# A decoder step on one core: the head that builds the modulated input is rebuilt, and index queries are projected only from token 256 on

## The chip, the core and the metric

The kernel runs on one core of a Trainium2 chip. Its time is the device time of one execution in microseconds (us). Before the change three runs gave a median of 1173.57 us, from 1172.87 to 1173.94. The engines are called PE (TensorE, matrix products), DVE (VectorE), ACT (ScalarE), POOL (GpSimd) and SP (SyncE, which issues nearly all DMAs). PSUM holds what PE writes, SBUF everything else. A line number such as L209 is a line of the kernel before; lines of the kernel after are always called so.

## The reference, cut to what matters

The step takes 1024 new prompt tokens and 8 sequences of 4 sample tokens, 1056 in all, each a row of 1024 values.

```
mod = silu(c) @ w_ada + b_ada                     # c: 9 conditioning rows
shift, scale, gate = split(mod, 3)
r = rsqrt(mean(x*x) + 1e-6)                       # one norm factor per token
h = (x * r) * g_norm * (1 + scale) + shift
qa, ka, va, za, qi, ki, wi, qr, kr, vr, zr, ga, gr = split(h @ w_in)
# index scores: sum over 4 heads of relu(qi . ki) * wi; 256 best keys per query, causal
# attention of qa over the chosen ka, va; times silu(za)
# retention (qr, kr with rotary, vr, decay per head, chunks of 128), group norm, times silu(zr)
merged = sigmoid(ga) * (y_a @ w_pa) + sigmoid(gr) * (y_r @ w_pr)
y = rms_norm(x + gate * (merged @ w_out), g_final)
```

A query at position below 256 has at most 256 admissible keys, so for it all of them are chosen and its index scores decide nothing. Sample tokens also take part, with 1024 cached keys and their own.

## The kernel before, in words

All of h is held transposed, channels on partitions, tokens along the row: 8 tiles of 128 channels (index k) by 1056 tokens. Each fp32 value is split into a high and a low part (`HH[k]`, `HL[k]`), and so is each weight (`wh`, `wl`). A projection of 128 output columns is, for each of 3 chunks of 352 tokens and each k, three products: wh·HH, wh·HL, wl·HH (`terms`, L206 to L211), 72 in all.

The stages are these. **The head** (L232 to L340) loads the constants `C` (128x792), the rows of x (one sample block, 8 prompt blocks) and the weights `wa` of the modulation, two 512 KB loads for each k. Each block of x is squared on ACT with a sum per row (L285); after three blocks a reciprocal root is taken on DVE, the block is scaled by it on DVE or POOL (L292), transposed on PE (L295) and copied from PSUM on ACT and DVE (L297). For each k `h_tile` multiplies the conditioning by `wa` (PE, L203), copies (ACT, L305), sums by another product (L308), forms scale AA and shift BB on DVE (L309, L310), applies them to the 1024 prompt columns in one instruction (L312) and to the 32 sample columns in two (L315), casts HH on ACT (L316) and subtracts for HL on DVE or POOL (L317). `start_two` runs inside that: two projections at once (index keys KI with the head weights, and the first 128 index query columns QI), 18 products for each k in six PSUM banks, with their weights split on POOL (L222, L223).

**The index stage** then copies these results out, transposes the keys (L627), projects the other 128 query columns (`project(O_QI + 128, ...)`), and scores queries from token 256 on against keys (L645, L646; combined on DVE, L652), then the sample tokens against the cache. ACT's copy L712 of the sample scores is the last input of the **selection**.

**The selection** (`pick_all`) searches a threshold bit by bit: 31 rounds in which DVE counts five blocks (L728) and ACT two (L735), with a few tiny DVE instructions per round (L742, L804, L806), followed by exact tie handling and a mask for each block (L780 to L784). It shares DVE with the gates' projections and with **retention**, four pairs of heads one after the other; each pair has a recurrence of seven DVE steps over S (L489), read by PE in L508. Attention for samples, attention for prompt tokens and the output follow.

The order on each engine is not written out: a scheduler simulates a timeline while the program is built and places instructions by it; pools with few buffers and `tc.issue_after` edges (an order on one engine, not a wait of its own) restrict it. At run time each engine works its list in that order.

Of the kernel before, what the change touches and what calls it, by code (L numbers as in the profile page):

```python
# [30 lines left out]
SQD = ()  # L31
SEQ = (8, 0, 1, 2, 3, 4, 5, 6, 7)
GRP = (0, 3, 6, 9)
CP = 0
PH = (2, 4, 6)
# [84 lines left out]
def _hybrid_step(ctx, tc, A, outs, dbg):  # L120
# [26 lines left out]
    nc.sync.dma_start(C, A["cst"])  # L147
# [34 lines left out]
    gT = cst.tile([128, 4], F32, name="gT")  # L182
    
# [15 lines left out]
    def ada_rows(x, w):  # L199

        for k in range(KT):
            q = k % 4
            nc.tensor.matmul(x[32 * q:32 * q + 32], scT[:, k], w[:, k], start=(k < 4), stop=(k >= 4))  # L203
# [11 lines left out]
    def start_two(pool, f0, f1):  # L215

        banks = [pj()[:, :CH] for _ in (0, 1)] + [x[:, o:o + CH] for x in (pl(), pl()) for o in (0, 512)]
        W = []
        for f in (f0, f1):
            ws = wload(wp, w_in, f, 128)  # L220
            wh, wl = [pool.tile([128, KT, 128], F32R, name="x", bufs=9) for _ in "hl"]
            nc.gpsimd.tensor_scalar(wh, ws, 1.0, 1.0, op0=OP.mult, op1=OP.mult)  # L222
            nc.gpsimd.tensor_sub(wl, ws, f32(wh))  # L223
            W.append((wh, wl))
        for k in range(KT):
            for i, p in enumerate(banks):
                terms(p, W[i // 3], k, chunks[i % 3])
        return banks
# [3 lines left out]
    with ExitStack() as s0:  # L232
        sp = s0.enter_context(tc.tile_pool(name="sp", bufs=1, reuse_waits="tile"))
        NWA = 5
        warm = sp.tile([1, 1], F32, name="warm")
        nc.vector.memset(warm, 0.0)
        nc.scalar.activation(warm, warm, AF.Tanh)
        craw, th = [sp.tile([128, D], F32, name="wa", bufs=NWA)[:9] for _ in (0, 1)]
        nc.scalar.dma_start(craw[0:1], A["c_prompt"])
        nc.scalar.dma_start(craw[1:9], A["c_sample"])  # L240
        rows = sp.tile([48, 128], F32, name="rows")
# [5 lines left out]
        ssq = sp.tile([128, 9], F32, name="ssq")  # L247
        nc.vector.memset(ssq, 1.0)
        XR = sp.tile([128, KT, TT], F32, name="xr")
        AA = sp.tile([128, KT, 9], F32, name="AA")  # L250
        BB = sp.tile([128, KT, 9], F32, name="BB")
        X = {}

        def x_load(t):
            n = 128 if t < 8 else NS
            X[t] = sp.tile([128, D], F32, name="x", bufs=9)
            nc.sync.dma_start(X[t][:n], xp[t * 128:t * 128 + 128] if t < 8 else xs)

        def cond():
# [11 lines left out]
            nc.vector.tensor_scalar(cols[:, 8:16], cols[:, 8:16], 1.0, None, op0=OP.add)  # L271
            nc.vector.tensor_copy(gT, cols[:, 32:36])

        def x_blocks(i0, i1):

            size = lambda t: 128 if t < 8 else NS
            for i in range(i0, i1):
                t = SEQ[i]
                n, x = size(t), X[t]
                sq = sp.tile([128, D], BF, name="sq", bufs=2)  # L280
                if t in SQD:
                    nc.vector.tensor_tensor_reduce(out=sq[:n], in0=x[:n], in1=x[:n], scale=1.0, scalar=0.0,
                                                   op0=OP.mult, op1=OP.add, accum_out=ssq[:n, i:i + 1])
                else:
                    nc.scalar.activation(sq[:n], x[:n], AF.Square, accum_out=ssq[:n, i:i + 1])  # L285
# [3 lines left out]
            for i in range(i0, i1):  # L289
                t = SEQ[i]  # L290
                n, x = size(t), X[t]
                (nc.vector if t % 2 else nc.gpsimd).tensor_scalar(x[:n], x[:n], r[:n, i - i0:i - i0 + 1], 1.0, op0=OP.mult, op1=OP.mult)  # L292
                p = pl().rearrange("p (k t) -> p k t", k=KT)
                for k in range(KT):
                    nc.tensor.transpose(p[:, k, :n], x[:n, 128 * k:128 * k + 128], ident[:n, :n])  # L295
                for g, copy in ((slice(0, 4), nc.scalar.copy), (slice(4, 8), nc.vector.tensor_copy)):
                    copy(XR[:, g, t * 128:t * 128 + n], p[:, g, :n])  # L297

        def h_tile(k, w2):

            pm = pt()
            for o, w in enumerate(w2):
                ada_rows(pm[:, 128 * o:128 * o + 128], w)
# [5 lines left out]
            nc.vector.tensor_scalar(AA[:, k], pm[:, 16:25], cols[:, 8 + k:9 + k], cols[:, 24 + k:25 + k], op0=OP.add, op1=OP.mult)  # L309
            nc.vector.tensor_scalar(BB[:, k], pm[:, 0:9], cols[:, k:k + 1], None, op0=OP.add)  # L310
            h = XR[:, k, :T]
            nc.vector.tensor_scalar(h, h, AA[:, k, 0:1], BB[:, k, 0:1], op0=OP.mult, op1=OP.add)  # L312
            hs = XR[:, k, T:].rearrange("p (b i) -> p b i", b=NB)
            for op, ab in ((OP.mult, AA), (OP.add, BB)):
                nc.vector.tensor_tensor(hs, hs, ab[:, k, 1:9].unsqueeze(2).to_broadcast([128, NB, NI]), op=op)  # L315
# [3 lines left out]
        wa = {}  # L319

# [983 lines left out]
```

## Time and profile before

| what | value |
|---|---|
| median of 3 runs | 1173.57 us |
| profiled execution, its own time | 1169.95 us |
| span of its trace | 1168.1 us |
| mean granted clock of TensorE | 0.98 |
| PE busy | 1104.2 us (95%) |
| DVE busy | 669.1 us (57%) |
| ACT busy | 452.8 us (39%) |
| POOL busy | 329.6 us (28%) |

The busy times are sums over a span of stages with different limits, and matmul records overlap, so PE's 95% says only that it is rarely without work. The profile's row of 40 slices shows for PE a 4 in the first slice and nines nearly everywhere else; DVE has nines and eights from the sixth slice to the fifteenth, and is far lower behind. The profiled execution is 3.6 us shorter than the median of the runs.

### The profile page before, as it was taken

To read this page: it belongs to the slowest core of one execution; us is meant where nothing else is said; L and a number is where in the kernel's file an instruction comes from. 1 tells how busy PE (TensorE), PEld (TensorE's weight loads), DVE (VectorE), ACT (ScalarE), POOL (GpSimd) and SP (SyncE) were. 2 spreads that over 40 slices of the span, in tenths; PEclk is the share of its full clock that TensorE was granted. 3 is DMA by queue.
4 is the path that set the end of the run, shared out by engine and by line. 5 is a ranking of instruction groups with operands and counts; after the bars stand their busy time and mean duration, and the time that the engine had idled before them with its cause. 6 is when DMAs were issued, how large, how long until landed. Compare 5 with 4: busy or idle time off the path is not lost. (4 is left out here: it accounts for less than half of the span.)

```text
span 1168.1 us, 20306 instructions
## 1 busy us (share of the span) xinstructions
PE 1104.2 (95%) x8040; PEld 1008.5 (86%) x8040; DVE 669.1 (57%) x1599; ACT 452.8 (39%) x874; POOL 329.6 (28%) x258
## 2 busy tenths in 40 slices
PE   4999999999989959999998999999999999989997
PEld 3899989999879959999998999877888888888786
DVE  6865349999999998113332222211237767477755
ACT  5465445555555311222243333212326666343211
POOL 2413006023311700160332222053114433376000
PEclk9999999999999987999999999999999999999999
DMA  9913234145222422341687567589889841395221
GB/s 306 255 33 109 74 105 139 38 126 140 84 79 93 148 58 80 101 120 29 220 269 237 178 205 213 154 294 305 266 245 237 233 135 55 123 299 176 106 97 54
DMA packets 157892, 181.51 MB, mean 155 GB/s; under 512 B 18837, under 2 KB 129501, under 8 KB 156710
## 3 DMA queue, kind: packets, MB, share of 16 engines
q1 hardware_dynamic: 147864, 144.51, 41.7%
q0 software_dynamic: 9856, 35.66, 9.2%
q8 instruction: 63, 1.03, 0.4%
q14 instruction: 31, 0.25, 0.1%
q10 hardware_dynamic: 78, 0.06, 0.0%
HBM read 137.81 MB, written 38.60 MB: 151 GB/s over the span
## 5 line engine op out<-in xcount | busy, mean ns | idle before, releaser
L209 PE MATMUL pj<-hh,wh 128*128 128x352 f32 x1176 | 387.7, 330 | 7.6 <-ACT kx L395 3.0
L211 PE MATMUL pj<-hh,wl 128*128 128x352 f32 x1176 | 383.1, 326 | 0.0
L210 PE MATMUL pj<-hl,wh 128*128 128x352 f32 x1176 | 382.6, 325 | 0.0
L209 PEld LDWEIGHTS pj<-hh,wh 128*128 128x128 f32 x1176 | 223.0, 190 | 17.1 <-issue 6.0
L210 PEld LDWEIGHTS pj<-hl,wh 128*128 128x128 f32 x1176 | 223.7, 190 | 3.3 <-issue 2.5
L211 PEld LDWEIGHTS pj<-hh,wl 128*128 128x128 f32 x1176 | 223.0, 190 | 3.9 <-issue 3.4
L728 DVE TENSOR_SCALAR_CACHE_REDUCE eq<-sc,cand 128x896 bf16<-128x896 f32 (+4 forms) x155 | 135.7, 875 | 2.3
L196 POOL TENSOR_TENSOR wl<-ws,wh 128x1024 fp32r<-128x1024 f32 (+1 forms) x33 | 63.6, 1930 | 190.9 <-ACT wh L195 172.6
L195 ACT CAST wh<-ws 128x1024 fp32r<-128x1024 f32 (+1 forms) x65 | 61.1, 940 | 108.4 <-PE pj L210 66.9
L196 DVE TENSOR_TENSOR wl<-ws,wh 128x1024 fp32r<-128x1024 f32 x32 | 39.9, 1247 | 86.8 <-ACT wh L195 86.8
L1065 POOL TENSOR_SCALAR lg<-lg,st 128x1024 f32<-128x1024 f32 (+7 forms) x64 | 47.5, 749 | 75.3 <-DVE st L1064 69.6
L735 ACT ACTIVATE ra<-sc,cand 128x1024 bf16<-128x1024 f32 x31 | 35.6, 1149 | 64.9 <-DVE cand L806 64.9
L911 POOL DMA_INDIRECT kv<-in_cache_k,idx x32 | 30.9, 966 | 102.0 <-PE str L941 84.0
L1063 ACT ACTIVATE lg<-lg,st 128x1024 f32<-128x1024 f32 (+7 forms) x64 | 49.5, 775 | 21.4 <-DVE st L1062 21.2
L943 DVE COPY kt<-str 128x512 f32<-128x512 f32 x32 | 22.1, 689 | 61.3 <-PE str L941 57.6
L911 POOL DMA_INDIRECT kv<-in_cache_v,idx x32 | 31.4, 981 | 71.0 <-PE sx L969 41.8
L1241 PE MATMUL pj<-wol,MH 128*128 128x512 f32 (+1 forms) x136 | 51.2, 377 | 0.0
L1240 PE MATMUL pj<-woh,MH 128*128 128x512 f32 (+1 forms) x136 | 51.2, 377 | 0.0
L1242 PE MATMUL pj<-woh,ML 128*128 128x512 f32 (+1 forms) x136 | 51.2, 377 | 0.0
L574 ACT ACTIVATE raw<-pj 128x352 f32<-128x352 f32 x48 | 22.1, 460 | 71.9 <-PE pj L211 68.7
L1078 PE MATMUL tr<-C,lg 128*128 128x128 f32 x288 | 43.8, 276 | 1.3 <-ACT pT L1080 0.5
L1078 PEld LDWEIGHTS tr<-C,lg 128*128 128x128 f32 x288 | 33.7, 140 | 8.7 <-ACT pT L1080 1.9
(337 smaller groups left out, 2055.6 us busy)
## 6 DMA issues: line engine op xcount, KB each, us to landing
ws<-in_w_in SPq DMA_DIRECT2D x51, 512.0 KB
TG<-raw SPq DMA_DIRECT2D x16, 528.0 KB
rot<-in_rot SPq DMA_DIRECT2D x8, 1056.0 KB
wa<-in_w_ada SPq DMA_DIRECT2D x16, 512.0 KB
u<-TG SPq DMA_DIRECT2D x8, 528.0 KB
RT<-u SPq DMA_DIRECT2D x8, 528.0 KB
t<-TG SPq DMA_DIRECT2D x8, 528.0 KB
u<-RT SPq DMA_DIRECT2D x8, 528.0 KB
```

Source lines behind the costliest of these rows:

```text
L195: nc.scalar.copy(wh[:, :, :n], ws[:, :, :n])
L196: (nc.vector if len(order) % 3 else nc.gpsimd).tensor_sub(wl[:, :, :n], ws[:, :, :n], f32(wh[:, :, :n]))
L209: nc.tensor.matmul(p, wh[:, k], HH[k][:, sl], start=(k == 0), stop=False)
L210: nc.tensor.matmul(p, wh[:, k], HL[k][:, sl], start=False, stop=False)
L211: nc.tensor.matmul(p, wl[:, k], HH[k][:, sl], start=False, stop=(k == KT - 1))
L728: nc.vector.tensor_scalar(junk[:n, :W], sc, thr[:n, j:j + 1], 0.0, op0=op, op1=OP.add, accum_out=cnt[:n, j:j + 1])
L911: nc.gpsimd.indirect_dma_start(out=t.rearrange("p s c -> p (s c)"), out_offset=None, in_=cache.rearrange("g (r s) h d -> (g r) (s h d)", s ...
L1063: nc.scalar.activation(l, l, AF.Exp, bias=st[:, 2:3], scale=0.125, accum_out=st[:, 3:4])
L1078: nc.tensor.transpose(x[:, 128 * (j - j0):128 * (j - j0) + 128], lg[:, j % 2, 128 * (j // 2):128 * (j // 2) + 128], ident)
L1240: nc.tensor.matmul(x, MH[:, k, tk], wh[:, k], start=(k == 0), stop=False)
L1241: nc.tensor.matmul(x, MH[:, k, tk], wl[:, k], start=False, stop=False)
L1242: nc.tensor.matmul(x, ML[:, k, tk], wh[:, k], start=False, stop=(k == KT - 1))
```

## The change

In the head, raw rows of x are transposed as they land and copied out unscaled. The squares are taken on ACT, except blocks 1 and 4, which DVE takes. The norm factors come in two groups (five blocks, then four); each is put on the diagonal of a 128x128 tile, and a product of a matrix of ones with that tile spreads it over all partitions into `RB`, so that norm and scale are applied to the transposed tile in one DVE instruction. The shift is added where HH is cast (ACT) and HL formed (DVE), each in two halves of 528 columns. AA and BB move to ACT. Nothing in the head runs on POOL. Of the constants only the identity is loaded ahead of x, the other 664 columns behind it. The weights of the two first projections are loaded behind the first pair of `wa` and split on ACT and DVE; later weights are ordered behind the last `wa` load and the last HH and HL. The six products of a term become five: three of 352 columns for KI, two of 400 for the queries (tokens 256 to 655, 656 to 1055), and a term runs over all five before the next. The second block of query columns uses the same two pieces.

```diff
-GRP = (0, 3, 6, 9)
-PH = (2, 4, 6)
+SQD = (1, 4)
-    nc.sync.dma_start(C, A["cst"])
+    nc.sync.dma_start(C[:, :C_CAUS], A["cst"][:, :C_CAUS])
+    late = [slice(256, 656), slice(656, TT)]
+    def start_two(W):
+        x, y = pl(), pl()
+        parts_ = [(p[:, :sl.stop - sl.start], sl, i) for p, sl, i in
+                  zip((pj(), pj(), x[:, :512], x[:, 512:], y[:, :512]), chunks + late, (0, 0, 0, 1, 1))]
         for k in range(KT):
-            for i, p in enumerate(banks):
-                terms(p, W[i // 3], k, chunks[i % 3])
+            for term in range(3):
+                for p, sl, i in parts_:
+                    nc.tensor.matmul(p, W[i][term == 2][:, k], (HL if term == 1 else HH)[k][:, sl], ...)
+        part = lambda: sp.tile([128, D], F32, name="x", bufs=11)
+        def x_block(i):
+            for k in range(KT):
+                nc.tensor.transpose(p[:, k, :n], x[:n, 128 * k:128 * k + 128], ident[:n, :n])
+            if t in SQD: nc.vector.tensor_tensor_reduce(out=sq[:n], in0=x[:n], in1=x[:n], ...)
+            else: nc.scalar.activation(sq[:n], x[:n], AF.Square, accum_out=ssq[:n, i:i + 1])
+            for g, copy in ((slice(0, 4), nc.scalar.copy), (slice(4, 8), nc.vector.tensor_copy)):
+                copy(XT[:, g, t * 128:t * 128 + n], p[:, g, :n])
+        def norms(i0, i1):
+            r = rsqrt(sp, v, i1 - i0)
+            for i in range(i1 - 4, i1):
+                nc.vector.tensor_scalar(dg, ident, r[:, i - i0:i - i0 + 1], None, op0=OP.mult)
+                nc.tensor.matmul(p[:, o:o + 128], one, dg, start=True, stop=True)
+            nc.scalar.copy(RB[:, c0:c0 + 512], p)
+            ...
-            h = XR[:, k, :T]
-            nc.vector.tensor_scalar(h, h, AA[:, k, 0:1], BB[:, k, 0:1], op0=OP.mult, op1=OP.add)
-            nc.scalar.copy(HH[k], XR[:, k])
-            (nc.gpsimd if k in PH else nc.vector).tensor_tensor(HL[k], XR[:, k], f32(HH[k]), op=OP.subtract)
+            nc.scalar.activation(AA[:, k], pm[:, 16:25], AF.Identity, bias=cg[:, k:k + 1], scale=cols[:, 24 + k:25 + k])
+            nc.scalar.activation(shift, pm[:, 0:1], AF.Identity, bias=cols[:, k:k + 1])
+            h = XT[:, k]
+            nc.vector.scalar_tensor_tensor(h[:, :T], h[:, :T], AA[:, k, 0:1], RB[:, :T], op0=OP.mult, op1=OP.mult)
+            for sl in (slice(0, 528), slice(528, TT)):
+                high = nc.scalar.activation(HH[k][:, sl], h[:, sl], AF.Identity, bias=shift)
+                rest = nc.vector.scalar_tensor_tensor(HL[k][:, sl], h[:, sl], shift, f32(HH[k][:, sl]), op0=OP.add, op1=OP.subtract)
+        nc.sync.dma_start(C[:, C_CAUS:], A["cst"][:, C_CAUS:])
+        for k in range(KT):
+            load_wa(k)
+            if k == 0:
+                for f in (O_KI, O_QI):
+                    with tc.issue_after(loads[-1].ins):
+                        ws = wload(wp, w_in, f, 128)
+                    nc.scalar.copy(wh, ws)
+                    nc.vector.tensor_sub(wl, ws, f32(wh))
+            head_ends = h_tile(k, modulation(k))
+            with tc.issue_after(loads[-1].ins), tc.issue_after(head_ends[0].ins), tc.issue_after(head_ends[1].ins):
+                split.append((f0, wsplit(wp, wload(wp, w_in, f0, 128), 128)))
-            project(O_QI + 128, use_qi(2))
+            project(O_QI + 128, use_qi(2), late)
```

On PE, where the first products of the projections stand: before, each row gives the line, the operation, what is written and read, and how often. `C` is the constant that sums the modulation (L308), `scT` the conditioning (L203), `hh_77` and `hl_85` are the high and low part of tile k = 0, `x` there the split weights.

```order
L295 MATMUL pl<-C,x 128x128 x8
L203 MATMUL pt<-wa,scT 32x128 x8
L308 MATMUL pt<-C,ar 128x16 x2
L203 MATMUL pt<-wa,scT 32x128 x16
L209 MATMUL pj<-hh_77,x 128x352 x2
L209 MATMUL pl<-hh_77,x 128x352 x2
L308 MATMUL pt<-C,ar 128x16 x2
L203 MATMUL pt<-wa,scT 32x128 x8
L210 MATMUL pj<-hl_85,x 128x352
L211 MATMUL pj<-hh_77,x 128x352
```

The same place after the change (the loads `wa` are called `x` in L202 of the kernel after, the weights `w`, and L224 is `start_two`).

```order
L302 MATMUL pj<-dg,one 128x128
L320 MATMUL pt<-C,ar 128x16 x2
L202 MATMUL pt<-x,scT 32x128 x16
L224 MATMUL pj<-hh_77,w 128x352 x2
L224 MATMUL pl<-hh_77,w 128x352
L224 MATMUL pl<-hh_77,w 128x400 x2
L320 MATMUL pt<-C,ar 128x16 x2
L202 MATMUL pt<-x,scT 32x128 x16
L224 MATMUL pj<-hl_85,w 128x352 x2
L224 MATMUL pl<-hl_85,w 128x352
L224 MATMUL pl<-hl_85,w 128x400 x2
```

The five high products of tile 0 now stand directly behind the 16 modulation products of k = 2, and its low products behind those of k = 3.

On SP, the order of loads at the start of the program, before.

```order
L147 DMA C<-in_cst 128x792
L257 DMA x<-in_x_sample 32x1024
L257 DMA x<-in_x_prompt 128x1024 x8
L323 DMA wa<-in_w_ada 128x8x128 x3
L189 DMA ws<-in_w_in 128x8x128 x2
L323 DMA wa<-in_w_ada 128x8x128 x6
L189 DMA ws<-in_w_in 128x8x128
```

And after; a load `x<-in_w_ada` is half of a tile's `wa`.

```order
L144 DMA C<-in_cst 128x128
L258 DMA x<-in_x_sample 32x1024
L258 DMA x<-in_x_prompt 128x1024 x8
L351 DMA C<-in_cst 128x664
L347 DMA x<-in_w_ada 128x8x128 x2
L188 DMA ws<-in_w_in 128x8x128 x2
L347 DMA x<-in_w_ada 128x8x128 x14
L188 DMA ws<-in_w_in 128x8x128 x2
```

Before, the first of the later weights was loaded behind nine halves of `wa`; now all 16 stand ahead of it, and the other 664 columns of constants stand behind x.

On DVE, the end of the recurrence of the third pair of retention (S) among the masks of the selection, before.

```order
L489 SCALAR_TENSOR_TENSOR S<-S,rc,pt 128x64
L783 SCALAR_TENSOR_TENSOR ra<-sc_773,base,ra 128x512
L780 TENSOR_SCALAR eq<-sc_774,base 128x640
L489 SCALAR_TENSOR_TENSOR S<-S,rc,pt 128x64
L393 TENSOR_TENSOR raw<-pj,raw 128x352
L784 TENSOR_SCALAR bi_763<-ra 128x512
L781 SCALAR_TENSOR_TENSOR ra<-eq 128x640
```

The same place after (L520 is the recurrence in the kernel after, L809 to L813 are the masks).

```order
L812 SCALAR_TENSOR_TENSOR ra<-sc_776,base,ra 128x512
L809 TENSOR_SCALAR eq<-sc_777,base 128x640
L520 SCALAR_TENSOR_TENSOR S<-S,rc,pt 128x64
L813 TENSOR_SCALAR bi_97<-ra 128x512
L520 SCALAR_TENSOR_TENSOR S<-S,rc,pt 128x64
L810 SCALAR_TENSOR_TENSOR ra<-eq 128x640
L424 TENSOR_TENSOR raw<-pj,raw 128x352
L520 SCALAR_TENSOR_TENSOR S<-S,rc,pt 128x64
```

The last step of S stood ahead of the mask of 512, the scan of 640 and the subtraction for `raw`; now it stands behind all three.

## Rows read from the trace of the kernel before

**Rows 1.** Windows by stage: stretch, length, busy (instructions) per engine, PE clock, DMA, GB/s.

```profile
core 0: us, PE busy (x) PEld busy (x) DVE busy (x) ACT busy (x) POOL busy (x), PEclk, DMA share, GB/s
0.00:70.00 70.00, 52.36 (x514) 47.04 (x515) 45.80 (x107) 31.69 (x53) 25.08 (x17) 0.98 0.86 236
70.00:161.00 91.00, 90.16 (x560) 79.59 (x558) 45.65 (x86) 48.90 (x84) 13.98 (x11) 1.00 0.24 74
161.00:440.00 279.00, 255.75 (x1817) 246.72 (x1817) 263.46 (x627) 133.66 (x237) 77.33 (x37) 0.97 0.36 104
440.00:1168.00 728.00, 705.94 (x5156) 635.19 (x5155) 314.17 (x781) 238.52 (x501) 213.17 (x193) 0.98 0.57 178
```

**Rows 2.** Waits of PE: line waited for, total us, times, longest.

```profile
PE pt L264 <- DVE wa L261: 13.7, 1, 13.7
PE pl L508 <- DVE S L489: 12.6, 1, 12.6
```

**Rows 3.** Timeline of PE and ACT: end of `start_two`, start of the selection.

```profile
69.93 0.38 PE L627 MATMUL pt<-C,kiT 128*128 128x128 f32 x2
161.08 1.00 ACT L712 COPY scs<-pl 32x1024 f32<-32x1024 f32 x1 [2.65 <-PE pl L710]
```

**Rows 4.** Timeline of ACT: squares of the first and third prompt blocks.

```profile
7.69 1.06 ACT L285 ACTIVATE sq<-x 128x1024 bf16<-128x1024 f32 x1 [1.47 <-DMA x<-in_x_prompt]
...
10.33 1.06 ACT L285 ACTIVATE sq<-x 128x1024 bf16<-128x1024 f32 x1 [0.15 <-DMA x<-in_x_prompt]
```

**Rows 5.** Windows of 2 us inside the head.

```profile
10.00:12.00 2.00, 0.00 (x0) 0.00 (x0) 1.48 (x9) 1.85 (x5) 0.00 (x0) 1.00 1.02 414
22.00:24.00 2.00, 1.51 (x7) 1.54 (x8) 1.83 (x9) 0.00 (x0) 0.00 (x0) 1.00 1.20 290
36.00:38.00 2.00, 0.65 (x21) 0.41 (x14) 2.00 (x6) 1.33 (x3) 0.00 (x0) 1.00 1.17 292
40.00:42.00 2.00, 2.00 (x9) 2.00 (x8) 2.00 (x3) 0.90 (x1) 1.99 (x1) 0.50 1.07 282
```

**Rows 6.** Timeline of PE: neighbouring products of 352 columns.

```profile
41.41 0.49 PE L209 MATMUL pl<-hh,x 128*128 128x352 f32 x1
41.70 0.49 PE L210 MATMUL pl<-hl,x 128*128 128x352 f32 x1
...
384.24 0.32 PE L209 MATMUL pj<-hh,wh 128*128 128x352 f32 x1
384.40 0.32 PE L210 MATMUL pj<-hl,wh 128*128 128x352 f32 x1
```

**Rows 7.** Timeline of PE: one tile's modulation between products.

```profile
58.12 0.51 PE L308 MATMUL pt<-C,ar 128*128 128x16 f32 x4
...
59.57 0.43 PE L209 MATMUL pl<-hh,x 128*128 128x352 f32 x1
```

**Rows 8.** Timeline of DVE and ACT: instructions of a tile and their like.

```profile
41.17 2.23 DVE L315 TENSOR_TENSOR xr<-xr,AA 128x32 f32<-128x32 f32 x1
...
59.01 0.18 DVE L315 TENSOR_TENSOR xr<-xr,AA 128x32 f32<-128x32 f32 x1
...
60.08 1.07 ACT L316 CAST hh<-xr 128x1056 fp32r<-128x1056 f32 x1
...
88.59 1.27 DVE L652 SCALAR_TENSOR_TENSOR sc<-rl,wsc,sc 128x1024 f32<-128x1024 f32 x1
```

**Rows 9.** Timeline of DVE: last step of S of the third pair and what follows.

```profile
439.78 0.27 DVE L489 SCALAR_TENSOR_TENSOR S<-S,rc,pt 128x64 f32<-128x64 f32 x1
439.97 0.52 DVE L393 TENSOR_TENSOR raw<-pj,raw 128x352 fp32r<-128x352 f32 x1
440.40 0.41 DVE L784 TENSOR_SCALAR bi<-ra 128x512 bf16<-128x512 f32 x1
440.85 1.49 DVE L781 TENSOR_TENSOR_SCAN ra<-eq 128x640 f32<-128x640 f32 x1
```

**Rows 10.** One line of the selection: times, ns min/median/max, first and last start.

```profile
L742 DVE TENSOR_SCALAR inc<-cnt x31: 158/172/2314, 173.4 to 386.0; 128x5 int32<-128x5 f32 x31
```

More of the change, by code (lines that the diff above doesn't have):

```diff
@@ L182, in _hybrid_step @@
     gT = cst.tile([128, 4], F32, name="gT")
+    BI = {b: selp.tile([128, (b + 1) * 128], BF, name=f"bi{b}") for b in range(8)}
+    BIS = selp.tile([NS, LK], BF, name="bis")
     def wcols(src, k, f0, n):
@@ L202, in ada_rows @@
             q = k % 4
-            nc.tensor.matmul(x[32 * q:32 * q + 32], scT[:, k], w[:, k], start=(k < 4), stop=(k >= 4))
+            nc.tensor.matmul(x[32 * q:32 * q + 32], scT[:, k], w(k), start=(k < 4), stop=(k >= 4))
     w_in = A["w_in"][0]
@@ L213, in _hybrid_step @@
     chunks = [slice(c * CH, c * CH + CH) for c in range(3)]
[L215 to L224, printed above, removed]
-        for k in range(KT):
-            for i, p in enumerate(banks):
-                terms(p, W[i // 3], k, chunks[i % 3])
-        return banks
+    late = [slice(256, 656), slice(656, TT)]
[3 more added lines that the diff above has]
+                  zip((pj(), pj(), x[:, :512], x[:, 512:], y[:, :512]), chunks + late, (0, 0, 0, 1, 1))]
+        for k in range(KT):
+            for term in range(3):
+                for p, sl, i in parts_:
+                    nc.tensor.matmul(p, W[i][term == 2][:, k], (HL if term == 1 else HH)[k][:, sl],
+                                     start=(k == 0 and term == 0), stop=(k == KT - 1 and term == 2))
+        return [p for p, sl, i in parts_]
     scT = cst.tile([128, KT, 32], F32, name="scT")
@@ L288, in x_blocks, with modulation @@
             r = rsqrt(sp, v, i1 - i0)
[L289 to L299, printed above, removed]
+            p, c0 = pj(), 128 * SEQ[i1 - 4]
+            for i in range(i1 - 4, i1):
+                dg = sp.tile([128, 128], F32, name="dg", bufs=3)
+                nc.vector.tensor_scalar(dg, ident, r[:, i - i0:i - i0 + 1], None, op0=OP.mult)
+                o = 128 * (i - i1 + 4)
+                nc.tensor.matmul(p[:, o:o + 128], one, dg, start=True, stop=True)
+            nc.scalar.copy(RB[:, c0:c0 + 512], p)
+            if i0 == 0:
+                p = pt()
+                dg = sp.tile([128, 128], F32, name="dg", bufs=3)
+                nc.vector.tensor_scalar(dg[:NS, :NS], ident[:NS, :NS], r[:NS, 0:1], None, op0=OP.mult)
+                nc.tensor.matmul(p[:, :NS], one[:NS], dg[:NS, :NS], start=True, stop=True)
+                nc.vector.tensor_tensor(XT[:, :, T:], XT[:, :, T:], p[:, :NS].unsqueeze(1).to_broadcast([128, KT, NS]), op=OP.mult)
+        def modulation(k):
             pm = pt()
-            for o, w in enumerate(w2):
-                ada_rows(pm[:, 128 * o:128 * o + 128], w)
+            for o in (0, 1):
+                ada_rows(pm[:, 128 * o:128 * o + 128], lambda c: wa[k][o][:, c])
             ar = sp.tile([128, 256], F32, name="ar", bufs=2)
@@ L325, in _hybrid_step, with load_wa @@
+        wa, loads = {}, []
+        def load_wa(k):
+            wa[k] = [part().rearrange("p (k f) -> p k f", f=128) for _ in (0, 1)]
+            for o, w in enumerate(wa[k]):
+                loads.append(nc.sync.dma_start(w, wcols(A["w_ada"][0], KT, 1024 * o + 128 * k, 128)))
         for t in SEQ:
             x_load(t)
-        for j in range(NWA - 2):
-            load_wa(j)
-        for i in range(len(GRP) - 1):
-            if i == CP:
-                cond()
-                for j in range(NWA - 2, NWA):
-                    load_wa(j)
-            x_blocks(GRP[i], GRP[i + 1])
@@ L344, in _hybrid_step @@
+        first = start_two(W)
     order = [O_QI + 128] + [O_GA + 128 * j for j in range(4)]
@@ L364, in project @@
         for c, sl in enumerate(chunks):
-            p = pj()[:, :CH]
+            p = pj()[:, :sl.stop - sl.start]
             for k in range(KT):
@@ L575, in gates @@
             nc.sync.dma_start(TG[128 * j:128 * j + 128], t)
-    BI = {b: selp.tile([128, (b + 1) * 128], BF, name=f"bi{b}") for b in range(8)}
-    BIS = selp.tile([NS, LK], BF, name="bis")
     k_out, v_out, ki_out, st_out, ks_out, vs_out, kis_out, sts_out = outs[2:]
```

91 lines of the change are left out of this document (47 added, 44 removed).

## Prediction

> **What bounds the kernel now.** I read the windows by stage first [rows 1]. Up to 70 us PE is busy for 52.4 of 70 us; from 70 to 161 for 90.2 of 91; from 161 to 440 for 255.8 of 279 while DVE is busy for 263.5; behind 440 for 705.9 of 728. So the head has idle time on PE, the index stage is PE's, the selection is DVE's, and the rest is PE's again. The waits of PE [rows 2] then show where its idle time lies: 13.7 us once at the start, before the conditioning arrives, and 12.6 us once at L508, where the third pair of retention wants its recurrence S. That second wait says that from the selection's start to that point DVE decides, not PE: a gain on PE counts there only if it lets the selection start earlier. The two marks that I move are the end of `start_two` at 69.9 and the selection's start at 161.1 [rows 3]; the third is the last step of S, which ends at 439.78 + 0.27 = 440.05 [rows 9].
>
> **The head's loads.** The first and third blocks of x are squared at 7.69 and 10.33 [rows 4], both started by their DMA: 1.32 us a block, so the eighth is there at 7.69 + 7 x 1.32 = 16.9. That is 414 GB/s [rows 5]. The 664 columns of constants, 128 x 664 x 4 = 340 kB, now stand behind x: 0.82 us, so x is complete at 16.1 and the constants at 16.9. A weight load of 524 kB moves at 290 GB/s [rows 5]: 1.81 us. A pair of `wa` then lands at 20.5, the two weights at 24.1, and the pairs for k = 1, 2, 3 at 27.7, 31.4 and 35.0, the last of all at 49.5. The later weights wait behind these; they are there by 53, before their use.
>
> **PE in the head.** PE executes in order, and the first five products of tile 0 stand behind the modulation of k = 2, its low-part products behind that of k = 3. A tile's modulation takes PE 59.57 - 58.12 = 1.45 us [rows 7], about 1.0 of it products with `wa`. So the first products start at 31.4 + 1.0 = 32.4, and after them PE waits for the loads of k = 3 and resumes at 35.0 + 1.0 = 36.0. From there loads are ahead by 3.6 us a tile or better, and PE has: 69 products of 352 columns at 384.40 - 384.24 = 0.16 us [rows 6], 11.0; 46 of 400 columns at 0.16 x 400/352 = 0.18, 8.3; four modulations at 1.45, 5.8; a last L308, 0.45. Sum 25.6, end at 61.6.
>
> Does something else hold a tile? PE needs 15 products, 2.5 us, and 1.45: 4.0 us. DVE needs one scalar-tensor-tensor instruction of 1024, 1.27 [rows 8], the low part in two halves, 1.27 x 1056/1024 + 0.18 for the second start = 1.5, and three small ones at 0.18 [rows 8]: 3.3 us. ACT needs the cast in two halves, 1.07 [rows 8] and another start, and three small ones, under 2.6 even at 0.4 each. PE is the fullest, by 0.7 us; DVE covers the edits of a tile at nothing as long as its small ones stay at 0.18. Squares, diagonals and the ones products (1056 columns, under a microsecond of PE) lie beside the loads up to 31.4.
>
> The clock: in 36 to 38 us PE was busy for 0.65 of 2 us, and from 40 to 42 the granted clock was 0.50 [rows 5], that is 1.2 GHz; there products stood 41.70 - 41.41 = 0.29 apart in place of 0.16 [rows 6]. The new order has a hole of about 1.9 us between the first five products and the next. The spell in the trace lasts about 3.4 us and cost 1.7. If it comes, part of it falls into the hole; I take 0.9 of 1.7 and put the end of the head at 62.5, with 60.5 and 64.5 as bounds. Against 69.9 that is -7.4.
> The Trainium skill, "TensorE: Matmul & The Clock Gate", Part 1 (the clock gate), says that the array falls to half rate after it was idle and returns once it is busy; the trace agrees with its granted clock of 0.50 and 1.00. By that rule alone the whole 1.7 us would be paid and the end would be 63.3; by the row of a fully granted clock it would be 61.6.
>
> **The index stage.** This is PE's [rows 1], so columns count. The second block of query columns falls from 72 x 0.16 = 11.5 us to 48 x 0.18 = 8.6: -2.9. By the built lists 16 products of 352 columns, 2.5 us, move from before the last score product to behind it: -2.5 for the selection's start, not for PE's total. Against that, ACT now has two casts of the later weights, about 1.07 each [rows 8], ahead of its copies of the keys. Cost between nothing (they are done before the products end) and 2.1; I take 0.8, because the casts stand directly behind the last high part and there are some 2.5 us of products after that. The selection then starts at 161.1 - 7.4 - 2.9 - 2.5 + 0.8 = 149.1, that is 12.0 earlier.
>
> **The selection.** DVE decides here, and it gets the same counts. But in its list the last step of S now stands behind the scan of 640 (1.49), the mask of 512 (0.41) and the subtraction for `raw` (0.52) [rows 9]: +2.4. Third S ends at 440.05 - 12.0 + 2.4 = 430.4, -9.6. What of PE? The head's 7.4 and, counted in the two built lists, 10,880 columns less up to L508 (10,880/352 x 0.16 = 4.9) bring it there 7.4 + 4.9 - 0.8 = 11.5 earlier, S is 9.6 earlier, and it waited 12.6 [rows 2]. So it waits for 12.6 + 11.5 - 9.6 = 14.5 us, and DVE remains the bound: PE's further gain is lost in this wait. From that point PE's two lists are the same, and nothing of the new order can give time back or take it.
>
> **Sum.** The profiled execution took 1169.95 (a span of 1168.1 and 1.85 around it): 1169.95 - 9.6 = 1160.4. The median of the runs is 3.6 above it, and carried over to that, 1173.57 - 9.6 = 1164.0.
>
> **Rivals.**
> B, the head runs warm and the selection is luckier. If the clock stays at 1.00 and the loads come as early as 414 GB/s permits (1.27 a load, the pair of k = 3 at 29.6), PE is never held and the head ends at about 59: -3.5, 1160.5. The selection can also lose collisions: L742 has a median of 172 ns and a sum far above it, with a longest of 2314 [rows 10], 2.14 us more than the median. Two collisions fewer give another -4.3: 1156.2. For it: loads without other traffic. Against: 290 GB/s in both windows of weights.
>
> C, DVE becomes the bound of the tiles. L315 took 2.23 us at 41.17 and 0.18 at 59.01 [rows 8]; at the first POOL was busy for 1.99 of 2 us [rows 5]. If the small instructions of a tile stay slow (one 2.05 longer), DVE needs 3.3 + 2.05 = 5.4 us a tile, and eight tiles from 27.7, when the second pair has landed, end at 71, no earlier than now: the head's 7.4 are gone, 1171.4. For it: DVE was busy for 2.00 of 2 in the windows from 36 on. Against: POOL has nothing left in the head, and its work there was what stood beside the long rows.
> The Trainium skill, "SBUF — State Buffer", section "Who interferes with whom", says that DVE and GpSimd share one pair of ports, held exclusively for a whole instruction. The rows on L315 agree; by that rule C can't occur, while in the selection, where POOL goes on, it can.
>
> D, slower: the selection meets POOL more often. POOL is busy for 77 of its 279 us [rows 1], on work that moves by up to 12 us against the rounds of DVE, and each collision of a tiny instruction (L742, L804, L806 stand between the counts, where nothing else can go on) adds 2.14 us [rows 10] to the one engine that decides. The gain of 9.6 is used up at 4.5 more collisions; six more make +12.8, 1164.0 + 12.8 = 1176.8. For it: their number is a matter of phase, and 31 rounds have 93 such places. Against: POOL has the same work, so the mean number should not change.
>
> E, the change doesn't do what it says: fewer columns and an earlier head free PE, but PE's list is held by copies out of PSUM, so that PE idles in the index stage for as long as it saved there (2.9 + 2.5): -4.2 is left, 1169.4. Against: 90.2 of 91 us busy, before.
>
> **How the numbers follow.** A 0.60 (own range 1160 to 1168: bounds of the head of 2 either way, of the casts -0.8 to +1.3, one collision of 2.1), B 0.18, C 0.07, D 0.08, E 0.07. The forecast is A's 1164.0. What a measurement of this kernel can tell from no change is about 0.2%, 2.35 us. Faster by more: A nearly whole, B, most of E, a little of C, 0.84. Within it: C's rest and a part of E and D, 0.08. Slower: most of D, 0.08. The range takes in B down to 1156.5 and C's and E's sides up to 1171: what lies below and above has about 0.2.
>
> **What would show it.** Right: the first product L224 at about 32.4 and a hole behind five of them; `start_two` ending at 60.5 to 64.5; L741, the copy of the sample scores of the kernel after, starting near 149; L520's last step of the third pair ending near 430; PE waiting there for 12 us or more; an equal stretch behind it. Wrong: a head above 68 with DVE full (C); long tiny instructions in the selection in larger number and its stretch over 285 us (D); PE idle in the index stage by more than 4 us (E); or PE no longer waiting for the third S, which would put the bound elsewhere.

## The result and the profile after

The kernel after took 1160.38 us in the median (1158.07 to 1162.57, four runs) beside 1173.22 for the kernel before: a ratio of 0.989, 95% interval 0.9869 to 0.9911, or 12.8 us. In a second comparison the ratio was 0.9906 (0.9882 to 0.9931), 11.0 us of 1171. The forecast was 9.6; the profiled execution, 1158.07 us with a span of 1156.3, is 11.9 below that of before. The sum came out nearly right partly by luck: head and index stage gave 5.2 us less than forecast, and the selection and the stretch behind it, where a loss and nothing were forecast, gave 7.3 more.

The windows by stage of the kernel after, from the end of `start_two` on and cut at its own marks, answer to [rows 1]; columns as there.

```profile
core 0: us, PE busy (x) PEld busy (x) DVE busy (x) ACT busy (x) POOL busy (x), PEclk, DMA share, GB/s
64.90:154.30 89.40, 86.91 (x520) 74.65 (x519) 46.15 (x84) 44.60 (x77) 11.42 (x11) 1.00 0.34 99
154.30:431.50 277.20, 258.43 (x1840) 248.82 (x1841) 264.28 (x630) 133.53 (x239) 78.70 (x38) 0.98 0.34 101
431.50:1156.30 724.80, 704.44 (x5149) 633.35 (x5147) 310.49 (x778) 238.63 (x501) 212.51 (x193) 0.99 0.58 178
```

The marks of [rows 3, 9] in the timeline of the kernel after: first products, the low-part products of tile 0, end of `start_two`, start of the selection, last step of the third S.

```profile
32.77 1.29 PE L224 MATMUL pj<-hh,w 128*128 128x352 f32 x2
...
37.49 0.96 PE L224 MATMUL pj<-hl,w 128*128 128x352 f32 x2
...
64.90 0.38 PE L656 MATMUL pt<-C,kiT 128*128 128x128 f32 x2
...
154.29 1.00 ACT L741 COPY scs<-pl 32x1024 f32<-32x1024 f32 x1 [4.08 <-PE pl L739]
...
431.24 0.27 DVE L520 SCALAR_TENSOR_TENSOR S<-S,rc,pt 128x64 f32<-128x64 f32 x1
```

| stretch | before | forecast | after |
|---|---|---|---|
| head, to the end of `start_two` | 69.9 | 62.5 | 64.9 |
| index stage, to the selection's start | 91.2 | 86.6 | 89.4 |
| selection's start to the end of the third S | 279.0 | 281.3 | 277.2 |
| from there to the end of the span | 728.0 | 728.0 | 724.8 |

So the selection started 6.8 us earlier, not 12.0, and the third S ended 8.5 us earlier, not 9.6. PE's waits still have that S at the top, with 9.1 us in place of 12.6 [rows 2]; the next row is the query tiles of the index stage.

```profile
PE pl L539 <- DVE S L520: 9.1, 1, 9.1
...
PE pl L674 <- DVE qs L639: 1.4, 2, 1.0
```

The last step of S is a mark, but not what PE waits for. The products read S of the chunk before, so the last state is none of theirs, and they start 0.15 us after the end of the step before the last, in both kernels: before at 438.88, after at 429.65, that is 9.2 us earlier. That step and the product, before and then after:

```profile
438.46 0.27 DVE L489 SCALAR_TENSOR_TENSOR S<-S,rc,pt 128x64 f32<-128x64 f32 x1
438.88 0.47 PE L508 MATMUL pl<-S,qrT 64*128 64x64 f32 x2 [12.62 <-DVE S L489]
```

```profile
429.23 0.27 DVE L520 SCALAR_TENSOR_TENSOR S<-S,rc,pt 128x64 f32<-128x64 f32 x1
429.65 0.48 PE L539 MATMUL pl<-S,qrT 64*128 64x64 f32 x2 [9.08 <-DVE S L520]
```

Windows inside the head of the kernel after, for [rows 5]: the granted clock is at its half level, 1.2 GHz, while the first products run (from 24.9 to 38.5), and full from there on.

```profile
24.00:26.00 2.00, 0.49 (x2) 0.30 (x2) 1.99 (x6) 0.69 (x3) 0.00 (x0) 0.72 1.17 291
32.00:34.00 2.00, 1.90 (x19) 1.09 (x9) 2.00 (x4) 2.00 (x4) 0.00 (x0) 0.50 1.15 288
36.00:38.00 2.00, 2.00 (x34) 1.54 (x27) 1.97 (x4) 0.47 (x3) 0.00 (x0) 0.50 1.10 282
40.00:42.00 2.00, 2.00 (x15) 2.00 (x13) 0.20 (x1) 0.00 (x0) 0.00 (x0) 1.00 1.16 294
```

And a wait that the forecast did not have. SP issues the page table only at 63.24, when the head's last low part is done, because the tile takes over memory of the head (with a tile of its own, below, it is issued earlier); on DVE the instruction that uses it (L692) waits until 74.93, with the query subtractions (L639) behind it, and PE waits for those three times. First SP, then DVE, then PE:

```profile
63.24 3.66 SPq L687 DMA_DIRECT2D ptab<-in_page_table  x8
...
74.93 0.17 DVE L692 TENSOR_SCALAR ptab<-ptab 128x8 int32<-128x8 int32 x1 [2.39 <-DMA sx<-in_sxc]
75.13 0.58 DVE L639 TENSOR_TENSOR qs<-pl,qs 64x400 fp32r<-64x400 f32 x1
...
75.77 0.50 PE L674 MATMUL pl<-kih,qs 128*128 128x512 f32 x1 [0.96 <-DVE qs L639]
78.98 0.40 PE L208 MATMUL pj<-hh,wh 128*128 128x352 f32 x1 [1.10 <-DVE qs L639]
85.23 0.47 PE L674 MATMUL pl<-kih,qs 128*128 128x512 f32 x1 [0.42 <-DVE qs L639]
```

The row of L692 names `sx`, a load issued at 67.42 behind the table; by the code L692 reads the table alone, and where the table is loaded earlier (below) the wait is gone with `sx` left where it was. From 64 to 72 next to nothing moves, with the table and, from 68.4 on, a 512 KB load outstanding:

```profile
68.00:70.00 2.00, 2.00 (x14) 1.96 (x14) 1.88 (x5) 1.92 (x5) 0.00 (x0) 1.00 0.05 0
...
74.00:76.00 2.00, 1.04 (x6) 0.70 (x5) 1.00 (x4) 0.56 (x2) 0.00 (x0) 1.00 1.08 319
```

### The profile page after: what moved, and what is told of

Same layout as the page of the kernel before. It is cut to its first block, busy times and chain, and to the rows that moved or that the text cites. A ratio compares the mean times of both kernels' runs of the same rounds, so it can differ in the third digit from the quotient of the medians.

```text
span 1156.3 us, 20264 instructions
## 1 busy us (share of the span) xinstructions
PE 1105.4 (96%) x8010; PEld 1006.7 (87%) x8010; DVE 664.5 (57%) x1599; ACT 454.8 (39%) x890; POOL 304.3 (26%) x246
## 5 line engine op out<-in xcount | busy, mean ns | idle before, releaser
L208 PE MATMUL pj<-hh,wh 128*128 128x352 f32 (+1 forms) x1168 | 384.6, 329 | 6.7 <-ACT qs L428 1.8
L210 PE MATMUL pj<-hh,wl 128*128 128x352 f32 (+1 forms) x1168 | 380.9, 326 | 0.0
L209 PE MATMUL pj<-hl,wh 128*128 128x352 f32 (+1 forms) x1168 | 379.3, 325 | 0.0
L208 PEld LDWEIGHTS pj<-hh,wh 128*128 128x128 f32 x1168 | 220.6, 189 | 18.4 <-issue 9.8
```

The lines of the kernel that those rows point to most:

```text
L208: nc.tensor.matmul(p, wh[:, k], HH[k][:, sl], start=(k == 0), stop=False)
L209: nc.tensor.matmul(p, wh[:, k], HL[k][:, sl], start=False, stop=False)
L210: nc.tensor.matmul(p, wl[:, k], HH[k][:, sl], start=False, stop=(k == KT - 1))
```

## The experiments

Ratios are to the kernel before, run beside it; the base is the kernel after in its second comparison, 0.9906. Against its first, 0.989, each gain over the base is 1.9 us smaller. Each trace is one execution.

**The kernel after once more.** No edit.

> The kernel after, unchanged, beside the kernel before on the chip on which the next ones run: the base for these, and a second profile of it. Theory: the 727 to 728 us behind the third S in four of five traces are the rule and the 724.6 of the first trace of the kernel after was a lucky wait for a row buffer, so its time here is some 3 us longer than 1156.3 by the span, and the ratio to before nearer to 0.991 than to 0.989. Rival (724.6 belongs to the change): the stretch behind the third S is 724.6 again.

Ratio 0.9906, 1161.03 us (1160.14 to 1166.07). The profiled execution was its longest. Its head ended at 64.07, the selection started at 153.44, S ended at 430.9; behind that it took 733.4 us where the first trace has 724.8. The ratio is as the theory had it; on the stretch both expectations miss, since it differs by 8.6 us between executions of one program. PE's waits behind 600 us name one place, 2.7 of the 8.6 us: gathered rows of the value cache. The granted clock was also at its half level for 33.7 us of this stretch, in the first trace for 21.6; what that costs was not tried by itself. The row of the wait in this trace, and then that of the first one:

```profile
PE sx L999 <- DMA kv<-in_cache_v,idx: 3.4, 2, 2.2
```

```profile
PE sx L999 <- DMA kv<-in_cache_v,idx: 0.7, 2, 0.4
```

So the 3.2 us that the first trace shows behind the third S are no part of the change's effect that these runs can establish.

**The second query block alone, in the kernel before.**

```diff
-            project(O_QI + 128, use_qi(2))
+            project(O_QI + 128, use_qi(2, late), late)
```

> The kernel before, with one part of the change alone: the second block of index query columns is projected from token 256 on (two pieces of 400 columns in place of three of 352); head and start_two as before. Theory (PE bounds the index stage, DVE the selection, and what comes earlier at the selection's start stays earlier): 24 x 0.16 us less on PE against 48 x 0.02 more for the wider pieces, 2.9 us, selection starts at 158.2 in place of 161.1 and the time falls by 2.9 to about 1170.3. Rival (the wait of 12.6 us for the third S swallows what PE saves, since DVE's work is the same): no change, 1173.2, with the selection starting where it did. Collisions of tiny DVE instructions with POOL can add or take 2.1 us each in either case.

Ratio 0.9964 (0.9949 to 0.998), 4.2 us: faster, and not less than the columns are worth. In the trace the selection started 2.8 us earlier, at 158.31, but the third S ended at 440.0, as before. The runs decide for the theory. In that one trace, 2 us above its own median, DVE took the gain back: up to the last round of the selection 3.3 us less than before, from there to the end of S 5.8 more, with 75 instructions in place of 69. Where the other executions kept it, no trace shows.

**The new head alone (all query columns).**

```diff
-                  zip((pj(), pj(), x[:, :512], x[:, 512:], y[:, :512]), chunks + late, (0, 0, 0, 1, 1))]
+                  zip((pj(), pj(), x[:, :512], x[:, 512:], y[:, :512], y[:, 512:]), chunks + chunks, (0, 0, 0, 1, 1, 1))]
-            project(O_QI + 128, use_qi(2), late)
+            project(O_QI + 128, use_qi(2))
```

> The kernel after, with the query columns undone: both blocks are projected for all 1056 tokens again, six pieces in start_two; the new head stays. Theory: 24 products of 352 come back in start_two and 24 in the second block, 2 x 2.9 us, so start_two ends at 64.9 + 2.9 = 67.8 and the time rises by 5.8 to about 1166.2; the new head alone is then worth some 7 us. Rival (in the new kernel the index stage is held by waits for DVE, not by columns): the second block's part is swallowed, time rises by 2.9 or less, 1160.4 to 1163.3.

Ratio 1.0003 (0.9984 to 1.0021): without the shorter queries the new head gives nothing. Both expectations miss by 6 us or more. `start_two` ended at 65.5, 4.4 earlier than before, but the selection started at 161.15, as before: the index stage ate it. DVE waited 3.24 us for the page table here, and PE 3.66 for the query tile behind it:

```profile
78.13 0.50 PE L674 MATMUL pl<-kih,qs 128*128 128x512 f32 x1 [3.66 <-DVE qs L639]
```

From 79.0 to 82.5 the clock then was at its half level. So the two parts of the change do not add up: the 48 products put back cost 11 us against the base, where 5.8 were expected. The index stage took 95.6 us, 6.2 more than in the kernel after; 2.9 of these are the columns of the second block by the expectation, 2.7 the longer wait for the query tile. Why that wait is longer here was not tried.

**The page table early.** It is loaded into the tile of the indices, behind the second pair of `wa`.

```diff
+            if k == 1:
+                for j in range(8):
+                    nc.sync.dma_start(gidx[16 * j:16 * j + 16], bass.AP(...page_table...))
-            nc.vector.tensor_scalar(ptab, ptab, 16, None, op0=OP.mult)
+            nc.vector.tensor_scalar(gidx, gidx, 16, None, op0=OP.mult)
```

> The kernel after, with the page table loaded straight into a tile of its own, early in the head, in place of a tile that takes over memory of the head and so can be loaded only when the last low part of h is done (issued from 63.2 us on, and DVE waits for it until 74.9 with the query subtractions queued behind). Theory (this wait of 2.4 us on DVE is why PE waits three times for the query tiles, 3.1 us against 0.95 before): PE's waits fall to about 1, the selection starts 2 us earlier, at 152.3, time 1158.4. Rival (the subtractions are late because ACT's casts are late): the waits stay, the selection starts at 154.3, time 1160.4.

Ratio 0.9952 (0.9932 to 0.9972), slower than the base. The index stage shortened as expected, from 89.4 to 87.6, but PE waited 4.46 us in the head for a pair of `wa`, since the eight small loads got between them, and `start_two` ended at 69.23. From 26 to 32 the DMA engines moved at most 12 GB/s, though two halves of `wa` had been issued by 28.6; in the kernel after they moved 290 there. The wait, and a window inside that hole:

```profile
35.34 1.08 PE L202 MATMUL pt<-x,scT 128*32 128x128 f32 x16 [4.46 <-DMA x<-in_w_ada]
```

```profile
28.00:30.00 2.00, 2.00 (x21) 1.30 (x20) 0.00 (x0) 0.37 (x1) 0.00 (x0) 0.50 0.05 0
```

**The page table behind the weights.** The same, at `k == KT - 1`, ordered behind the last `wa`.

> The kernel after, with the page table loaded into a tile of its own, all eight pieces ordered behind the last modulation weights on SP (in the run with the early table they stood among the weights and made PE wait 4.5 us for a pair); PE, ACT and POOL keep their order. Theory: the head ends at 64.9 as in the kernel after, the three waits for query tiles fall from 3.1 to about 1.5 us and the selection starts some 1.8 us earlier, time lower by 1.8. Rival (with or without that wait the end of the third S is set by the rounds and their collisions): selection earlier but the end within 1 us.

Ratio 0.9884 (0.9858 to 0.991), 1159.42 us. Head 65.4, selection at 153.04: the index stage took 87.6 us, 1.8 less than in both traces of the base, and the waits for query tiles are 0.56 and 0.44. That part of the theory is shown. The time is 2.6 us below the base by the ratios, with intervals that overlap.

**Throwaway products in the head**, nine, then three.

```diff
+            if k < 3:
+                idle = pj()
+                for _ in range((4, 4, 1)[k]):
+                    nc.tensor.matmul(idle, one, XT[:, 7, :512], start=True, stop=True)
```

> The kernel after, with nine throwaway products of 128x128 by 512 columns on PE in the head, four ahead of each of the first two tiles' modulation and one ahead of the third, written to a PSUM bank that nobody reads. Theory (the granted clock of 0.50 from 25.1 to 38.8 us makes the first tiles late by some 2.4 us): the clock stays at 1.00 from about 25 on, start_two ends near 62.5 in place of 64.9, time 1158 if the gain lasts to the end. Rival (the first tiles are held by the loads, which are 3.6 us apart, and the clock costs nothing there): start_two ends at 64.9 or later, by as much as the throwaway work stands in the way (0.85 us each at the full clock), time 1160.4 to 1163.

> The kernel after, with three throwaway products of 512 columns in the head (two after the first tile's modulation, one after the second's) in place of the nine that stood in the way. Three profiles of the same head so far ended it at 65.1, 64.3 and 62.4 us with half spells of 13.7, 13.7 and 3.4 us. Theory (the half spell costs the head its 2 to 3 us): the spell is 3.4 us or gone and the head ends at 62.4 or earlier, time about 2 us lower than the kernel after, 1159. Rival (three products in the way cost as much as the clock gives): the head ends at 64 to 66, no change, 1161.

With (4, 4, 1) the half spell shrank to 3.4 us, but the products took 0.92 us each at the full clock, the first useful ones started at 36.4, and `start_two` ended at 68.0: ratio 0.9938 (0.9918 to 0.9958), 3.7 us above the base, with intervals that overlap a little. With (2, 1, 0) it ended at 63.3, 1.6 and 0.7 earlier than in the two traces of the base, ratio 0.987 (0.9847 to 0.9893): lower than the base, but the intervals overlap.

**Filling PE's wait for the third S.**

```diff
+                for _ in range(36):
+                    with tc.issue_after(last.ins):
+                        last = nc.tensor.matmul(idle, HH[0][:, :128], HH[1][:, :512], start=True, stop=True)
```

> The kernel after, with 36 throwaway products of 512 columns (high parts of h, full rate, about 0.22 us each, 7.9 us in all) on PE ahead of the third pair's products with S, where PE waits 9.1 us for DVE; written to a PSUM bank that nobody reads. Nothing that DVE does is changed. Theory (the idle wait drops the granted clock to 0.50 from 424.5 to 444.9, and the 13.5 us of work behind it take twice their time): S ends where it did, the clock stays at 1.00 behind it, and the time falls by 6 to 7 us, to about 1154. Rival (the clock falls whatever PE does there, or what follows waits for DVE anyway): no change, 1160 to 1161.

Ratio 0.9973 (0.9953 to 0.9993): 7.8 us slower than the base. The edit missed its place. The scheduler put the 36 products at 409.8, ahead of projections that had stood before the wait, and 43 of these went behind it; PE still waited, 7.5 us, and the clock fell. The run says nothing of the clock, but that 8.6 us of PE work in this stretch cost nearly as much. Its head, however, is the same list as the kernel after on PE, ACT and DVE, and in it the clock fell for 3.4 us only: full in the window where it was half above, and `start_two` ended at 62.17.

```profile
32.00:34.00 2.00, 1.56 (x9) 1.32 (x9) 2.00 (x5) 1.70 (x4) 0.00 (x0) 1.00 1.14 287
...
62.17 0.38 PE L664 MATMUL pt<-C,kiT 128*128 128x128 f32 x2
```

**The third S ahead of the masks**, of the last four, then of all but the first.

```diff
+                    if W in (512, 640, 768, 896):       # then: if W != LK
+                        s4.enter_context(tc.issue_after(chain[2].ins))
```

> The kernel after, with the masks of the last four blocks of the selection ordered behind the third pair's recurrence S on DVE, in place of among its steps; same instructions. Theory (DVE's order at this place decides, and the half clock follows from the wait): S ends some 6 us earlier, PE's wait falls from 9.1 to 3 or less, the clock stays up or its half spell is short: 6 us by the wait and up to 6 by the clock, time 1148 to 1154. Rival (the next thing that PE needs, a raw subtraction or the masks, is then late instead): the wait moves behind, gain of 2 us or less, 1158 or more.

> The kernel after, with all masks of the selection except the first (the one of the samples) ordered behind the third pair's recurrence S on DVE, so that S no longer stands behind the scans of 1024 and 384, which kept its first step until 422 us in the run with only the last four masks moved. Theory (DVE's order at this place is what PE waits for, 9.1 us, and the half clock from 424 to 445 follows from that wait): S ends near 417, before PE gets there at about 419, the wait is gone and so is the half spell of 20 us: 9 us and some 6, time near 1146 to 1149 where the kernel after has 1161. Rival (DVE is what is short, and each us saved at S is waited for at the next place where PE wants DVE): the gain stays below 3 us, 1158 or more.

Behind the last four masks only, nothing was gained: ratio 0.9908 (0.9884 to 0.9931). S ended at 427.6, 3.9 and 3.3 earlier than in the two traces of the base, but the step that PE waits for came only 2.2 and 1.6 earlier, and PE also came to it 1.9 and 1.2 earlier, with 18 projection products fewer done, and waited 8.7 us. Behind all but the first, S ended at 416.9, PE waited 0.71 us, and the ratio was 0.9847 (0.9822 to 0.9871): 6.9 us below the base (5.0 by the first comparison), about half of what was expected. The clock still fell, from 419.6 to 429.9, though PE had hardly waited, and 24 products (3.9 us) had moved behind S.

**Table and S together, and all three.**

> Both edits together: the page table in a tile of its own behind the modulation weights, and all masks but the first behind the third pair's S. Theory: the gains add, since one lets the selection start earlier and the other takes the wait at its end: 1.6 us less than with the masks alone, 1144 to 1148. Rival (once PE no longer waits for S, what the index stage gives is PE's own gain and counts in full, or it is swallowed by DVE's rounds): between 0 and 3 us less than with the masks alone.

> The three edits that each gave a lower time than the kernel after, together: three throwaway products in the head, the page table behind the modulation weights, and all masks but the first behind the third pair's S. Theory (the three act at three places, and since PE no longer waits for the third S, what the head gives counts in full): some 2 to 3 us below the two edits without the head's, near 1149, with the head ending at 63.6 or earlier. Rival (the head's gain is a matter of the clock's phase in that run, or is waited for in the rounds of the selection, which DVE decides): 1151 to 1154.

The two together: 1152.18 us, ratio 0.9822 (0.9799 to 0.9846), the lowest of all, though above the 1144 to 1148 expected; it is 2.9 us below the masks alone, with intervals that overlap, so that the gains add is not shown. With the throwaway products added: 0.9884 (0.9863 to 0.9906), 7 us worse. The head ended at 63 and the selection started earlier by nearly 2, but the scheduler built another order: PE ran the same products between the selection's start and S in another sequence, stood before S at 409.8 and waited 6.14 us. The same products after S, first in the version with the two, where PE waited 0.97 us and the clock was full, then in the one with all three, where it was at its half level:

```profile
416.65 1.78 PE L545 MATMUL pl<-S,qrT 64*128 64x64 f32 x28 [0.97 <-DVE S L526]
418.36 3.79 PE L548 MATMUL pl<-vtok,tmp 128*128 128x64 f32 x32
```

```profile
415.95 3.25 PE L549 MATMUL pl<-S,qrT 64*128 64x64 f32 x28 [6.14 <-DVE S L530]
419.13 7.09 PE L552 MATMUL pl<-vtok,tmp 128*128 128x64 f32 x32
```

Windows from 416 to 428 of the two, in the same order: the granted clock is 1.00 and 0.50.

```profile
416.00:428.00 12.00, 9.44 (x93) 9.01 (x95) 11.72 (x17) 1.37 (x2) 0.00 (x0) 1.00 0.32 82
```

```profile
416.00:428.00 12.00, 12.00 (x69) 11.70 (x70) 11.68 (x15) 1.37 (x2) 0.00 (x0) 0.50 0.27 77
```

## Why the prediction was right, and which of its steps were not

**The loads and the first products: right, but without the hole.** The forecast was 32.4 from the pair of k = 2 at 31.4; it was 32.77. The wait for the loads of k = 3, up to 36.0, did not come: from the first product to the end of `start_two` PE stood idle for 0.2 us in all, for ACT. The low-part products followed at 37.49, since the modulation between ran at the half clock; in the run that was to fill PE's wait, where the clock was full here, at 35.21.

**The end of the head: the term for the clock was too small.** It was 0.9 us for a spell of 3.4; the spell was 13.7 us, and the end 64.9 in place of 62.5, just outside the stated bounds. Seven traces have this head with the same order on PE, ACT and DVE, and in them the end follows the half level behind the first product, whatever stood ahead of it:

| run | half level ahead of the first product | behind it | end of the head |
|---|---|---|---|
| filling PE's wait | 3.4 | 0 | 62.17 |
| S ahead of all masks but the first | 8.7 | 1.5 | 62.67 |
| the kernel after once more | 8.9 | 4.8 | 64.07 |
| the kernel after | 7.9 | 5.7 | 64.90 |
| table and S together | 7.4 | 6.2 | 64.95 |
| page table behind the weights | 6.8 | 6.8 | 65.40 |
| S ahead of the last four masks | 3.4 | 6.8 | 65.42 |

Each microsecond at the half level behind the first product cost about half a microsecond (3.2 us of end for 6.8); ahead of it, where the loads set PE's pace, up to 8.9 us of it cost nothing that shows. So the forecast's term was 0.9 us for what came to 2.7. What makes the spell late or long in one execution is not shown. Without it the head ended at 62.17, forecast 61.6, and that agreement is partly luck: the low-part products came 0.8 us earlier than forecast, and what follows them took 27.0 us in place of 25.6. For the tiles the working held: from the second tile on a tile took 4.1 us of PE, forecast 4.0. DVE as the bound of the tiles (the forecast's third case, C) did not occur.

**The index stage: the added wait was the wrong one.** The 0.8 us for ACT's casts stood for a wait that didn't matter. What came in was the page table: its tile lies in memory of the head, the load moved behind the last weights, and DVE, which executes in order, held the query subtractions behind it. PE's three steps to products that waited are 3.1 us longer than the normal step in total, against 0.95 for the one wait before; with the table loaded ahead of need the stage lost 1.8 of its 89.4 us. The lists of loads ahead of the prediction end before this load. The step that failed was to ask only what the moved weights wait for, and not which loads stand behind them and which queue waits for those. The forecast's last rival, PE idle in the index stage, so came true in part, for another reason and for 2.1 of its 5.4 us. The stage gave 1.8 us in place of 4.6. Of the 2.8 us between, the waits are 1.3 (2.1 in place of 0.8); the 40 products fewer gave 4.2 us, not 5.4; the products of the sample scores took 0.8 longer; and the rest 0.5 less.

**The selection: DVE decides, as forecast, and the 2.4 us for the new order came, but the rounds became shorter.** The stretch became 1.8 us shorter, 277.2 us, in the second trace of the kernel after 277.4. Cut at the end of the last round, it is two stretches: up to there 227.4 us before, 223.2 and 223.4 after; from there to the last step of S 51.5 before, 54.0 in both traces after, so 2.5 longer. The last round, before and then after:

```profile
388.35 0.17 DVE L804 TENSOR_TENSOR base<-base,inc 128x7 int32<-128x7 int32 x1
```

```profile
377.34 0.17 DVE L833 TENSOR_TENSOR base<-base,inc 128x7 int32<-128x7 int32 x1
```

The term was right, but it was laid on a step that PE does not wait for; the step before the last now stands behind the mask of 512 and what was ahead of that, and came 1.8 us later behind the last round. The 4.2 us of the rounds, which only rival B had, from two collisions fewer, are DVE's: it sat idle for 2.6 us less and was busy for 1.6 less. The rival of more collisions did not come about: of the 92 tiny instructions of the lines L742, L804 and L806, 10 took longer than 0.9 us before and 9 after. Why DVE idled less was not tried. The one line of [rows 10] again, in the kernel after, has the same median and about the same longest.

```profile
L771 DVE TENSOR_SCALAR inc<-cnt x31: 152/172/2409, 165.0 to 377.1; 128x5 int32<-128x5 f32 x31
```

That collisions are with POOL was not tried by itself.

**PE's gain lost at the third S: right, and it can be got back.** PE waited 9.1 us there, fewer than the 14.5 forecast, because it arrived 5.7 us earlier than before, not 11.5: head and index stage had given 5.2 us less. The step of S that it needs came 9.2 earlier, near the 9.6 that the forecast had for the last step. With S ahead of the masks the wait fell to 0.7 and the time by 6.9 us. The forecast did not see that the wait also costs behind its end: the clock was at its half level from 429.1 to 453.0 in the kernel before and from 424.2 to 444.7 in the kernel after. It fell during the wait and rose only 14.1 and 15.0 us after PE had started again, so the S products and their followers take 10.3 us there, against 5.5 at the full clock in the version with table and S together. That the wait alone makes the spell is not shown: with a wait of 0.7 us there still was one of 10.2 us.
The Trainium skill, "TensorE: Matmul & The Clock Gate", Part 1, says that the array idles down to half rate and comes back once it is busy; the fall to 0.50 in these waits agrees, and the return to 1.00 came, but late, 14.1 and 15.0 us into the work.

**Behind the third S: equal, as far as can be told.** 724.8 and 733.4 us in two executions of the kernel after stand on either side of 728.0 before. That the profiled execution gained 11.9 us and not some 8.5 is due to this stretch, and so to luck.

## What to carry to other kernels

When loads are re-ordered or pools re-cut, list every small load that then stands behind them, and who sits in an in-order queue behind its first reader: here a small table took back 1.8 of the 5.0 us that the new head gave. Look up which step of a chain the waiting engine reads, not only where the chain ends. A long wait of PE (6 to 13 us here) is priced with the half clock around it; it was removed here by the order of the engine waited for. Throwaway work and added edges change a scheduler's whole order: read where they landed before reading the time.

## What the runs showed of the hardware that was not expected

The half level in a head with one and the same order on PE, ACT and DVE lasted 3.4 us in one execution and 13.7 in others, and only its part behind the first product moved the end of the head, from 62.17 to 65.42. Behind the third S the clock rose only 14 to 15 us after PE had started again. Eight loads of the page table (16 x 8 numbers of 4 bytes each) stopped the stream of 512 KB loads behind them: from 26 to 32 us at most 12 GB/s in place of 290, with PE waiting 4.5 us for a pair. Issued alone from 63.2 to 66.9, they held DVE until 74.9, and the load of 512 KB issued at 68.4 did not move before 72.
